# Splitting the low parts of the last stage's weights between VectorE and GpSimd

## The chip, the cores and the metric

The kernel runs on one core of a Trainium2 chip. The metric is the device time of one execution in microseconds (us), the median over runs. Engines are named as the profile names them: PE is TensorE's matrix multiply and PEld its weight load, DVE is VectorE, ACT is ScalarE, POOL is GpSimd, SP is SyncE. In the trace each engine's instructions start in the order of its own list, so one that waits for another engine holds up everything behind it in that list.

## What is computed

One layer of a bidirectional encoder: an input projection, windowed attention, a bidirectional state-space scan, and then the last stage, which the change touches. Cut to that stage (x, h, attn, y and z_ssm come from the stages before; S = 2048 rows, D = 1024):

```python
y = jax.nn.gelu(y)
y = y * jax.nn.sigmoid(jnp.einsum('bsc,ce->bse', y, w_glu[l]) + b_glu[l])
ssm = y * jax.nn.silu(z_ssm)
merged = jax.nn.sigmoid(g_attn) * jnp.einsum('bsc,cd->bsd', attn, w_branch_attn[l]) \
       + jax.nn.sigmoid(g_ssm) * jnp.einsum('bsc,cd->bsd', ssm, w_branch_ssm[l])
x = x + jnp.einsum('bsd,de->bse', merged, w_out[l])
return rms_norm(x, final_norm_gain)
```

## The kernel before, in words

Every product is made in three passes (`mm3`, from line 218). Each operand is split into a high part, which is the value rounded to the matrix type, and a low part, which is the value minus the high part; then high times high, low activation times high weight, and high activation times low weight are added in one PSUM bank (lines 221, 222, 223). So every weight that PE uses needs a high part `wh` and a low part `wl` first. `split_w` (line 158) makes them: a DMA on SP's queue brings a tile `raw` of 128 x 1024, ACT copies it to `wh` (line 164), and `low_part` (line 150) subtracts `wh` from `raw` into `wl`. Before the change `low_part` does that on GpSimd in four instructions of 128x256 (line 156), except for the very first weight of the last stage, which VectorE does in one of 128x1024. There are two `raw` buffers and three pairs of `wh` and `wl`.

The last stage runs over four blocks of 512 rows in the order 2, 3, 1, 0; the text calls them the first, second, third and last block. A block has three parts.

- `glu`: four groups of 12 matmuls with `w_glu`, each followed by elementwise work on VectorE (`g`, `g`, `ta`, `sl`) and ACT (`ta`, `sh`).
- `branch`: for each e from 0 to 7 two groups of 12 matmuls, n = 0 with the attention weights (`ah`, `al`, bank `pj`) and n = 1 with the state-space weights (`sh`, `sl`, bank `s`). One weight tile holds both: its first half (columns k 0 to 3) is n = 0's, its second half n = 1's. After a group VectorE takes its bank out into a gate tile `gt` (line 1435); after n = 1 it adds the two (`m`, line 1439), ACT makes `mh` (line 1440) and VectorE the low part `ml` (line 1448).
- `outp`: eight groups of 24 matmuls with the output weight `woh`, `wol`, each followed by the residual add `xr` on VectorE (line 1491), then the final norm and the store.

The order is written out by hand. `wahead` (line 210) keeps the split weights ahead of PE: in `branch` the weight of e + 2 is split right behind the group (e, 0). While a branch runs, a side generator, `gelu_prep`, prepares the next block's `gh` and `gl` one step per group: a load of `yt` by ACT's DMA queue, a square on ACT (line 1321), a multiply on VectorE (line 1325), a tanh on ACT (line 1329), a multiply on VectorE (line 1333), the copy `gh` on ACT (line 1334) and the low part `gl` on VectorE (line 1338). The next block's `glu` needs all four `gl`. The last block has no such side work.

The output weight has two halves of 512 columns. The first is split before the first `glu`. The second is split inside the first block's `branch` in eight pieces (`wo_split`, line 1161): ACT makes `woh` and, as `WOP` is 1, GpSimd makes `wol` in two instructions of 128x256 (line 1173).

Of the kernel before, what the change touches and what calls it, by code (L numbers as in the profile page):

```python
# [7 lines left out]
F32 = mybir.dt.float32  # L8
# [4 lines left out]
ALU = mybir.AluOpType  # L13
# [6 lines left out]
KD = 8  # L20
# [7 lines left out]
RATE2 = 1.237  # L28
RATE3 = 1.499
WLAG = 2  # L30
WOP = 1
GELU_Q = 0.044715 ** 0.5
SCAN_SLOT = 0.994
FIRST = 1.711
# [4 lines left out]
def kernel(  # L39
# [10 lines left out]
    V, A, Q, PE = nc.vector, nc.scalar, nc.gpsimd, nc.tensor  # L50
# [49 lines left out]
    HALF = "half"  # L100
# [3 lines left out]
    def later(n, f):  # L104
        laters.append((n, f))
# [44 lines left out]
    def low_part(eng, lo, r, hi):  # L150

        n = lo.shape[1]
        step = max(1, n // 4) if eng is Q else n
        for k in range(0, n, step):
            ks = slice(k, k + step)
            eng.tensor_tensor(lo[:, ks], r[:, ks], hi[:, ks].bitcast(F32), ALU.subtract)  # L156

    def split_w(key, kt, cols, tag="w", bufs=3, eng=Q):
        r = wraw.pop(key)
        res = []  # L160
        for nm in ("h", "l"):
            t = wp.tile([128, KD, 128], F32R, tag=tag + nm, name=tag + nm, bufs=bufs)
            res.append(t.rearrange("p k c -> p (k c)")[:, 0:kt * cols].rearrange("p (k c) -> p k c", k=kt))
        A.activation(res[0], r, AF.Copy)  # L164
        low_part(eng, res[1], r, res[0])
        return res

    witems = []
    wsplit = []
    wpos = {"load": 0, "split": 0, "lag": WLAG}  # L170

    def wload_to(i):
        while wpos["load"] <= min(i, len(witems) - 1):
            r = wp.tile([128, KD, 128], F32, tag="raw", name="raw", bufs=2)
            it = witems[wpos["load"]]
            k0 = 0
            if it[0] == "h":
                nc.sync.dma_start(out=r.rearrange("p k c -> p (k c)").rearrange("p (k c) -> p k c", k=2),
                                  in_=hS[it[1], :, it[2]:it[2] + 2])
            elif it[0] == "wo":  # L180
                wo_load(0, it[1], r.rearrange("p k c -> p (k c)").rearrange("p (k c) -> p k c", k=2))
            for src in it[:0 if it[0] in ("wo", "h") else len(it)]:
                kt = src.shape[0] // 128
                nc.sync.dma_start(out=r[:, k0:k0 + kt], in_=src.rearrange("(k p) c -> p k c", p=128))
                k0 += kt
            wraw[wpos["load"]] = r
            wpos["load"] += 1

    def wsplit_next():
        j = wpos["split"]  # L190
        wload_to(j)
        it = witems[j]
        if it[0] == "h":
            h_split(it[1], it[2], wraw.pop(j).rearrange("p k c -> p (k c)").rearrange("p (k c) -> p k c", k=2))
        elif it[0] == "wo":
            wo_split(0, it[1], wraw.pop(j).rearrange("p k c -> p (k c)").rearrange("p (k c) -> p k c", k=2), V)
        else:
            wsplit.append(split_w(j, KD, 128, eng=V if j == wpos["glu"] else Q))
        wpos["split"] += 1
        if wpos["lag"]:  # L200
            later(wpos["lag"], lambda: wload_to(j + 2))
        else:
            wload_to(j + 2)
# [6 lines left out]
    def wahead(n):  # L210
        while len(wsplit) < n and wpos["split"] < len(witems):
            wsplit_next()

    def wpre():
        wload_to(1)
        wsplit_next()
# [921 lines left out]
    with tc.manual_schedule():  # L1138
# [11 lines left out]
        def h_split(b, k, r):  # L1150
            if k == 0:
                hblk[b] = [hp.tile([128, KD, BLK], F32R, tag=t, name=t) for t in ("hh", "hl")]
            hh, hl = hblk[b]
            ks = slice(k, k + 2)
            A.activation(hh[:, ks], r, AF.Copy)
            for j in range(2):
                for c in range(2):
                    cs = slice(c * 256, (c + 1) * 256)
                    Q.tensor_tensor(hl[:, k + j, cs], r[:, j, cs], hh[:, k + j, cs].bitcast(F32), ALU.subtract)

        def wo_split(n, k, r, eng):
            if (0, n) not in wo:
                wo[0, n] = hp.tile([128, KD, BLK], F32R, tag="hh", name="woh")
                wo[1, n] = hp.tile([128, KD, BLK], F32R, tag="hl", name="wol")
            ks = slice(k, k + r.shape[1])
            A.activation(wo[0, n][:, ks], r, AF.Copy)
            if eng is V:
                V.tensor_tensor(wo[1, n][:, ks], r, wo[0, n][:, ks].bitcast(F32), ALU.subtract)
                return
            for j in range(r.shape[1]):  # L1170
                for c in range(2):
                    cs = slice(c * 256, (c + 1) * 256)
                    Q.tensor_tensor(wo[1, n][:, k + j, cs], r[:, j, cs], wo[0, n][:, k + j, cs].bitcast(F32), ALU.subtract)
# [25 lines left out]
        def wsplit1(key):  # L1199
            if len(wt) < 3:  # L1200
                wt[key] = split_w(key, KD, 128)
                return
            r = wraw.pop(key)
            th = wI.tile([128, KD, 128], F32R, name=f"wh{key[0]}{key[1]}")
            tl = wI.tile([128, KD, 128], F32R, name=f"wl{key[0]}{key[1]}")
            A.activation(th, r, AF.Copy)
            low_part(Q, tl, r, th)
            wt[key] = (th, tl)
# [213 lines left out]
        def branch(b, nxt):  # L1422
# [6 lines left out]
            for e, n in seq:  # L1429
# [22 lines left out]
                if b == BO[0]:  # L1452
# [4 lines left out]
                    elif sl % 4 >= 2:  # L1457
                        k = sl // 4 * 2 + sl % 4 - 2
                        wo_split(1, k, wor[:, k % 2:k % 2 + 1], Q if WOP else V)
                if (e, n) == (1, 0):  # L1460
# [90 lines left out]
        for b in (2, 3, 0, 1):  # L1551
            for n, (key, w) in enumerate(zip(shared, ws)):
                for _ in range((2, 1, 1)[n] if b in (3, 0) else b == 1 and n == 1):
                    wsplit_next()
                proj(key[0], key[1], b, w)
# [82 lines left out]
```

## Time and profile before

| what | value |
|---|---|
| median of 3 runs | 1527.67 us (1526.7 to 1529.14) |
| the profiled execution | 1530.28 us, of which its span is 1528.5 us |
| PE busy | 1423.8 us, 93% of the span |
| DVE busy | 1027.4 us, 67% |
| ACT busy | 644.7 us, 42% |
| POOL busy | 629.1 us, 41% |
| mean granted TensorE clock | 0.975 |
| the last stage | from about 1087 us to the end |

The page counts busy time by engine over the whole span. The last stage is 441 us of it; of GpSimd's 380 weight instructions of line 156, 156 start there. Shares over the span say little about a stage: the views below are taken for stretches of it.

### The profile page before, as it was taken

How to read it: one execution, taken by the hardware profiler on the slowest of the kernel's cores; microseconds unless marked ns; L12 is line 12 of the kernel's file. 1: busy time of each engine (PE TensorE's matmuls, PEld its weight loads, DVE VectorE, ACT ScalarE, POOL GpSimd, SP SyncE). 2: the span in 40 equal slices, each digit the busy share in tenths (PEclk: the TensorE clock that was granted, in tenths of full speed). 3: DMA queues.
4: the chain of work that ended last, by engine and by line, in shares of the span. 5: the costliest groups of instructions: out<-in, count | busy, mean ns of one | idle time of the engine just before them, and what ended most of it. 6: DMA issues, size and time to landing. Idle time of an engine off the chain costs nothing.

```text
span 1528.5 us, 20091 instructions
## 1 busy us (share of the span) xinstructions
PE 1423.8 (93%) x6933; PEld 1154.0 (75%) x6933; DVE 1027.4 (67%) x2145; ACT 644.7 (42%) x1165; POOL 629.1 (41%) x887
## 2 busy tenths in 40 slices
PE   7999959988899999799999999999988998999998
PEld 6787747767777777688878888888766786877886
DVE  3325607899889998927888988863577376386442
ACT  6332123343344434424666666654444143243111
POOL 5520366966777861723111111113367053153320
PEclk9999979999999999999999999999999999999999
DMA  7443212232232233454323233235576376375341
GB/s 263 152 109 89 77 62 87 85 98 87 74 106 94 89 100 97 148 153 133 94 87 94 90 101 94 89 111 154 179 205 183 120 186 180 111 187 182 111 125 69
DMA packets 240727, 185.51 MB, mean 121 GB/s; under 512 B 57921, under 2 KB 202433, under 8 KB 240625
## 3 DMA queue, kind: packets, MB, share of 16 engines
q10 hardware_dynamic: 108336, 100.61, 22.5%
q1 hardware_dynamic: 132288, 83.62, 18.4%
q8 instruction: 54, 0.88, 0.2%
q14 instruction: 49, 0.39, 0.1%
HBM read 126.56 MB, written 57.62 MB: 121 GB/s over the span
## 4 chain that ended last, share of the span: by engine, by line
PE 46%; DVE 19%; DMA 8%; POOL 6%; issue 5%; ACT 4%; ACTq 0%; SPq 0%; POOLq 0%; DVEq 0%
PE pj L221 9%; PE pj L223 9%; PE pj L222 9%; DVE Hl L811 3%; PE s L1484 3%; PE s L1485 3%; PE s L1486 3%; PE s L1055 2%; PE s L1002 2%; PE s L1039 2%; DMA yt<-yS 2%; POOL wl L156 2%; DMA ar<-aS 2%; DVE ft L784 1%; DVE fu L785 1%
## 5 line engine op out<-in xcount | busy, mean ns | idle before, releaser
L156 POOL TENSOR_TENSOR wl<-raw,wh 128x256 fp32r<-128x256 f32 x380 | 329.8, 899 | 597.8 <-ACT wh L164 586.2
L221 PE MATMUL pj<-hh,wh 128*128 128x512 f32 x976 | 395.4, 405 | 0.0
L223 PE MATMUL pj<-hh,wl 128*128 128x512 f32 x976 | 387.5, 397 | 5.3 <-POOL wl L156 5.3
L222 PE MATMUL pj<-hl,wh 128*128 128x512 f32 x976 | 386.8, 396 | 0.0
L223 PEld LDWEIGHTS pj<-hh,wl 128*128 128x128 f32 x976 | 186.5, 191 | 48.2 <-POOL wl L156 6.6
L221 PEld LDWEIGHTS pj<-hh,wh 128*128 128x128 f32 x976 | 187.6, 192 | 36.7 <-issue 3.6
L222 PEld LDWEIGHTS pj<-hl,wh 128*128 128x128 f32 x976 | 187.5, 192 | 33.8
L164 ACT ACTIVATE wh<-raw 128x1024 fp32r<-128x1024 f32 x96 | 100.7, 1051 | 19.9 <-DMA raw<-in_w_branch_ssm_dram 5.7
L1484 PE MATMUL s<-woh,mh 128*128 128x512 f32 x256 | 101.9, 398 | 6.4 <-DVE xr L1491 6.4
L1486 PE MATMUL s<-woh,ml 128*128 128x512 f32 x256 | 101.3, 396 | 0.0
L1485 PE MATMUL s<-wol,mh 128*128 128x512 f32 x256 | 101.2, 395 | 0.0
L405 ACT ACTIVATE st<-pj,bg 128x512 f32<-128x512 f32 x64 | 44.0, 687 | 98.7 <-PE pj L223 86.8
L1019 ACT ACTIVATE p<-p,sml 128x384 f32<-128x384 f32 (+1 forms) x128 | 75.8, 595 | 17.4 <-DVE sml L1015 17.4
L1042 ACT ACTIVATE ph<-s 128x512 fp32r<-128x512 f32 x92 | 54.3, 590 | 57.5 <-PE s L1039 57.5
L1528 POOL TENSOR_TENSOR sm<-sm,mhalf 128x1 f32<-128x1 f32 x15 | 8.3, 553 | 170.3 <-DVE sm L1527 133.7
L1003 DVE CUSTOM_DVE_ANT_0 p<-s,bias 128x384 f32<-128x384 f32 (+1 forms) x128 | 68.3, 533 | 12.6 <-PE s L1002 12.0
L1044 DVE TENSOR_TENSOR pl<-s,ph 128x512 fp32r<-128x512 f32 x92 | 63.2, 687 | 19.2 <-ACT ph L1042 17.8
L1491 DVE TENSOR_TENSOR xr<-xr,s 128x512 f32<-128x512 f32 x32 | 21.9, 684 | 68.9 <-PE s L1486 68.9
L1484 PEld LDWEIGHTS s<-woh,mh 128*128 128x128 f32 x256 | 48.1, 188 | 20.4 <-DVE xr L1491 9.1
L1002 PE MATMUL s<-kst,qs 128*128 128x384 f32 (+1 forms) x256 | 61.7, 342 | 0.6 <-issue 0.6
L1039 PE MATMUL s<-ident,p 128*128 128x128 f32 x368 | 57.6, 274 | 0.0
L1039 PEld LDWEIGHTS s<-ident,p 128*128 128x128 f32 x368 | 46.4, 140 | 14.7 <-DVE p L1031 2.2
(277 smaller groups left out, 3038.5 us busy)
## 6 DMA issues: line engine op xcount, KB each, us to landing
raw<-in_w_in_dram SPq DMA_DIRECT2D x59, 512.0 KB
gS<-st ACTq DMA_DIRECT2D x64, 256.0 KB
gt<-gS ACTq DMA_DIRECT2D x64, 256.0 KB
x<-in_x_dram SPq DMA_DIRECT2D x16, 512.0 KB
raw<-in_w_branch_attn_dram SPq DMA_DIRECT2D x32, 256.0 KB
raw<-in_w_branch_ssm_dram SPq DMA_DIRECT2D x32, 256.0 KB
out_dram<-xr ACTq DMA_DIRECT2D x15, 512.0 KB
xr<-in_x_dram SPq DMA_DIRECT2D x12, 512.0 KB
```

What stands on the lines that cost most here:

```text
L156: eng.tensor_tensor(lo[:, ks], r[:, ks], hi[:, ks].bitcast(F32), ALU.subtract)
L164: A.activation(res[0], r, AF.Copy)
L221: PE.matmul(pt, w[0][:, k], r[0][:, k], start=start and k == 0, stop=False)
L222: PE.matmul(pt, w[0][:, k], r[1][:, k], start=False, stop=False)
L223: PE.matmul(pt, w[1][:, k], r[0][:, k], start=False, stop=stop and k == kt - 1)
L1002: PE.matmul(pt[:, 0:w], s["qs"][:, h], kst[:, r, kv, k0 * 128:k1 * 128], start=r == 0, stop=r == 1)
L1003: V.tensor_tensor_reduce(out=p[:, h, 0:w], in0=pt[:, 0:w], in1=bias[:, kv * 4 + h, r0:r1:-1], scale=1.0, scalar=0.0, op0=ALU.add, op1=ALU. ...
L1019: A.activation(p[:, h, 0:w], p[:, h, 0:w], AF.Exp, bias=nm[:, j:j + 1], accum_out=den[:, j:j + 1])
L1039: PE.transpose(pt[:, h * 128:(h + 1) * 128], s["p"][:, h, i * 128:(i + 1) * 128], ident)
L1484: PE.matmul(pt, mh[k][:, ts_], wo[0, n][:, k], start=k == 0, stop=False)
L1485: PE.matmul(pt, mh[k][:, ts_], wo[1, n][:, k], start=False, stop=False)
L1486: PE.matmul(pt, ml[k][:, ts_], wo[0, n][:, k], start=False, stop=k == KD - 1)
```

## The change

`low_part` gets a third kind, "half": VectorE subtracts the first half of the tile in one instruction of 128x512, and GpSimd the second half in two of 128x256. All weights of the last stage behind the first one are made that way (39 tiles: one of `w_glu` in the first block, two in each other, and eight of the branch weights in each of the four). `WOP` becomes 0, so that VectorE makes the eight pieces of the output weight's second half, in one instruction of 128x512 each.

```diff
-WOP = 1
+WOP = 0
...
         n = lo.shape[1]
-        step = max(1, n // 4) if eng is Q else n
-        for k in range(0, n, step):
+        if eng is HALF:
+            ks = slice(0, n // 2)
+            V.tensor_tensor(lo[:, ks], r[:, ks], hi[:, ks].bitcast(F32), ALU.subtract)
+        step = max(1, n // 4) if eng is not V else n
+        for k in range(n // 2 if eng is HALF else 0, n, step):
             ks = slice(k, k + step)
-            eng.tensor_tensor(lo[:, ks], r[:, ks], hi[:, ks].bitcast(F32), ALU.subtract)
+            (V if eng is V else Q).tensor_tensor(lo[:, ks], r[:, ks], hi[:, ks].bitcast(F32), ALU.subtract)
...
-            wsplit.append(split_w(j, KD, 128, eng=V if j == wpos["glu"] else Q))
+            wsplit.append(split_w(j, KD, 128, eng=V if j == wpos["glu"] else HALF if j > wpos["glu"] else Q))
```

Lines from 160 on stand three lines later in the changed file. The lists of PE, ACT and SP hold the same instructions in the same order as before; those of VectorE and GpSimd change.

VectorE in the second block's branch, from the bank of (2, 0) on. In the names, `gt` with `pj` is the bank of an n = 0 group taken out, with `s1` that of an n = 1 group; `yt` and `gl` are the side work for the next block. Before:

```order
L1435 SCALAR_TENSOR_TENSOR gt_11959<-gt_11959,pj_11999 128x512
L1338 TENSOR_TENSOR gl_11902<-yt_11903,gh_11901 128x512
L1435 SCALAR_TENSOR_TENSOR gt_11961<-gt_11961,s1_12025 128x512
L1439 TENSOR_TENSOR m_12041<-gt_11959,gt_11961 128x512
L1448 SCALAR_TENSOR_TENSOR ml_11884<-m_12041,mh_11876 128x512
L1325 SCALAR_TENSOR_TENSOR yt_11905<-yt_11905 128x512
L1435 SCALAR_TENSOR_TENSOR gt_11994<-gt_11994,pj_12049 128x512
L1333 SCALAR_TENSOR_TENSOR yt_11905<-yt_11905 128x512
```

The same place now:

```order
L1438 SCALAR_TENSOR_TENSOR gt_11937<-gt_11937,pj_11976 128x512
L155 TENSOR_TENSOR wl_11993<-raw_11916,wh_11992 128x512
L1341 TENSOR_TENSOR gl_11881<-yt_11882,gh_11880 128x512
L1438 SCALAR_TENSOR_TENSOR gt_11939<-gt_11939,s1_12001 128x512
L1442 TENSOR_TENSOR m_12017<-gt_11937,gt_11939 128x512
L1451 SCALAR_TENSOR_TENSOR ml_11863<-m_12017,mh_11855 128x512
L1328 SCALAR_TENSOR_TENSOR yt_11884<-yt_11884 128x512
L1438 SCALAR_TENSOR_TENSOR gt_11971<-gt_11971,pj_12025 128x512
L155 TENSOR_TENSOR wl_12042<-raw_11949,wh_12041 128x512
L1336 SCALAR_TENSOR_TENSOR yt_11884<-yt_11884 128x512
```

Behind each bank of an n = 0 group VectorE now has a low part, which reads the `wh` that ACT has still to make; everything below it, the side work among it, comes after.

ACT's list at the same place, which is unchanged (rows of the changed program; DMA issues stand among them):

```order
L1337 ACTIVATE gh_11880<-yt_11882 128x512
L167 ACTIVATE wh_11992<-raw_11916 128x1024
L1324 ACTIVATE yt_11884<-yt_11884 128x512
L1443 ACTIVATE mh_11855<-m_12017 128x512
```

`wh` stands behind `gh`, which itself reads the `yt` that VectorE made just before. GpSimd in the first block's branch, before:

```order
L156 TENSOR_TENSOR wl_11107<-raw_10968,wh_11106 128x256 x4
L1173 TENSOR_TENSOR wol_11140<-wor_11090,woh_11139 128x256 x2
L156 TENSOR_TENSOR wl_11145<-raw_11001,wh_11144 128x256 x4
L1173 TENSOR_TENSOR wol_11140<-wor_11090,woh_11139 128x256 x2
L156 TENSOR_TENSOR wl_11200<-raw_11113,wh_11199 128x256 x4
```

and now:

```order
L159 TENSOR_TENSOR wl_11104<-raw_10966,wh_11103 128x256 x2
L159 TENSOR_TENSOR wl_11140<-raw_10998,wh_11139 128x256 x2
L159 TENSOR_TENSOR wl_11193<-raw_11109,wh_11192 128x256 x2
L159 TENSOR_TENSOR wl_11244<-raw_11145,wh_11243 128x256 x2
L159 TENSOR_TENSOR wl_11299<-raw_11198,wh_11298 128x256 x2
```

The pieces of the output weight are gone from GpSimd, and two of four instructions of each weight; VectorE's list there has a `wol` and a `wl` more for each e.

## Rows read from the trace of the kernel before

**Rows 1.** The page's first section: busy us (share of the span) and number of instructions of each engine.

```profile
PE 1423.8 (93%) x6933; PEld 1154.0 (75%) x6933; DVE 1027.4 (67%) x2145; ACT 644.7 (42%) x1165; POOL 629.1 (41%) x887
```

**Rows 2.** The windows view of three branches (first, second and last block): the stretch, its length, then busy us and number of instructions of PE, PEld, DVE, ACT and POOL, then the granted clock, the DMA share and GB/s.

```profile
1113.00:1165.00 52.00, 45.74 (x176) 33.67 (x176) 39.70 (x43) 25.74 (x37) 41.96 (x45) 0.95 0.77 205
...
1222.00:1271.00 49.00, 46.13 (x196) 36.20 (x195) 37.56 (x45) 21.68 (x27) 26.92 (x32) 1.00 0.73 180
...
1434.00:1478.00 44.00, 44.00 (x191) 35.33 (x190) 23.58 (x33) 10.89 (x15) 20.82 (x25) 1.00 0.64 167
```

**Rows 3.** The waits view of PE from 1085 us to the end: who waited for whom, us in total, times, longest.

```profile
PE s L1484 <- DVE xr L1491: 6.4, 6, 2.0
PE pj L222 <- DVE gl L1338: 4.5, 3, 1.6
PE pj L221 <- ACT wh L164: 3.8, 6, 1.2
PE pj L223 <- POOL wl L156: 2.7, 2, 1.3
```

**Rows 4.** The same view and stretch for PE's weight loads.

```profile
PEld pj L223 <- POOL wl L156: 6.3, 7, 1.8
```

**Rows 5.** The timeline of VectorE in the second block's branch: start us, us, instruction, number, and in brackets the idle time before it and what ended it. Only some rows of the stretch.

```profile
1236.33 0.67 DVE L1435 SCALAR_TENSOR_TENSOR gt<-gt,pj 128x512 f32<-128x512 f32 x1
...
1242.76 0.68 DVE L1435 SCALAR_TENSOR_TENSOR gt<-gt,pj 128x512 f32<-128x512 f32 x1
...
1255.22 0.68 DVE L1435 SCALAR_TENSOR_TENSOR gt<-gt,pj 128x512 f32<-128x512 f32 x1
...
1261.75 0.69 DVE L1448 SCALAR_TENSOR_TENSOR ml<-m,mh 128x512 fp32r<-128x512 f32 x1 [3.40 <-ACT mh L1440]
1262.36 1.08 DVE L1325 SCALAR_TENSOR_TENSOR yt<-yt 128x512 f32<-128x512 f32 x1
1263.36 0.67 DVE L1435 SCALAR_TENSOR_TENSOR gt<-gt,pj 128x512 f32<-128x512 f32 x1
1264.14 1.05 DVE L1333 SCALAR_TENSOR_TENSOR yt<-yt 128x512 f32<-128x512 f32 x1
...
1268.86 0.68 DVE L1338 TENSOR_TENSOR gl<-yt,gh 128x512 fp32r<-128x512 f32 x1
```

**Rows 6.** The timeline of ACT in the same stretch, the weight copies and one row of the side work.

```profile
1237.03 1.05 ACT L164 ACTIVATE wh<-raw 128x1024 fp32r<-128x1024 f32 x1
...
1243.41 1.05 ACT L164 ACTIVATE wh<-raw 128x1024 fp32r<-128x1024 f32 x1
...
1255.94 1.04 ACT L164 ACTIVATE wh<-raw 128x1024 fp32r<-128x1024 f32 x1
1260.07 1.12 ACT L1321 ACTIVATE yt<-yt 128x512 f32<-128x512 f32 x1 [3.09 <-DMA yt<-yS]
...
1264.01 1.04 ACT L164 ACTIVATE wh<-raw 128x1024 fp32r<-128x1024 f32 x1
```

**Rows 7.** The timeline of PE at the seam between the second block's branch and the third block's glu.

```profile
1265.11 0.50 PE L221 MATMUL pj<-gh,wh 128*128 128x512 f32 x1 [1.23 <-ACT wh L164]
...
1269.60 0.51 PE L222 MATMUL pj<-gl,wh 128*128 128x512 f32 x1 [1.56 <-DVE gl L1338]
```

**Rows 8.** The view of one line, for three lines: instructions, duration in ns as least/median/most, first and last start, form.

```profile
L156 POOL TENSOR_TENSOR wl<-raw,wh x380: 718/747/1790, 9.9 to 1466.8; 128x256 fp32r<-128x256 f32 x190
...
L1439 DVE TENSOR_TENSOR m<-gt x32: 691/926/1279, 1116.7 to 1477.7; 128x512 f32<-128x512 f32 x32
...
L1448 DVE SCALAR_TENSOR_TENSOR ml<-m,mh x32: 691/1144/1154, 1120.0 to 1479.1; 128x512 fp32r<-128x512 f32 x32
...
L1435 DVE SCALAR_TENSOR_TENSOR gt<-gt,s x32: 671/680/689, 1116.0 to 1477.0; 128x512 f32<-128x512 f32 x32
```

**Rows 9.** The lines view of VectorE from 1222 to 1271 us (second block's branch): group, number, busy us, mean ns of one, idle before.

```profile
L1439 DVE TENSOR_TENSOR m<-gt 128x512 f32<-128x512 f32 x8 | 8.0, 1005 | 0.3
L1448 DVE SCALAR_TENSOR_TENSOR ml<-m,mh 128x512 fp32r<-128x512 f32 x7 | 7.1, 1014 | 7.7 <-ACT mh L1440 7.7
...
L1325 DVE SCALAR_TENSOR_TENSOR yt<-yt 128x512 f32<-128x512 f32 x4 | 4.9, 1226 | 0.0
L1333 DVE SCALAR_TENSOR_TENSOR yt<-yt 128x512 f32<-128x512 f32 x4 | 4.9, 1216 | 0.2
```

**Rows 10.** The same view from 1113 to 1165 us (first block's branch).

```profile
L1448 DVE SCALAR_TENSOR_TENSOR ml<-m,mh 128x512 fp32r<-128x512 f32 x8 | 8.5, 1063 | 9.1 <-ACT mh L1440 9.1
L1439 DVE TENSOR_TENSOR m<-gt 128x512 f32<-128x512 f32 x8 | 8.2, 1025 | 0.3
...
L1333 DVE SCALAR_TENSOR_TENSOR yt<-yt 128x512 f32<-128x512 f32 x4 | 5.4, 1355 | 0.2
L1325 DVE SCALAR_TENSOR_TENSOR yt<-yt 128x512 f32<-128x512 f32 x4 | 5.4, 1342 | 0.0
...
L1338 DVE TENSOR_TENSOR gl<-yt,gh 128x512 fp32r<-128x512 f32 x4 | 4.2, 1055 | 0.3 <-ACT gh L1334 0.3
```

**Rows 11.** The timeline of PE in the first block's branch, at a wait for a low part and behind it.

```profile
1138.30 0.64 PE L223 MATMUL pj<-ah,wl 128*128 128x512 f32 x1 [1.35 <-POOL wl L156]
1138.74 0.63 PE L221 MATMUL pj<-ah,wh 128*128 128x512 f32 x1
...
1141.73 0.48 PE L222 MATMUL pj<-al,wh 128*128 128x512 f32 x1
1142.05 0.40 PE L223 MATMUL pj<-ah,wl 128*128 128x512 f32 x1
1142.28 0.40 PE L221 MATMUL s<-sh,wh 128*128 128x512 f32 x1
```

## The prediction

> **What bounds the kernel now.** The page's first section comes first: over the span PE is busy 93% of the time, VectorE 67% and GpSimd 41% [rows 1]. These are averages, so the next view is the windows view of three branches [rows 2]. A branch is 16 groups of 12 matmuls; in the last block, where PE has no gap, it takes 44.0 us for 191 recorded matmuls, 0.23 us each. The first branch takes 52 us and the second 49. So PE loses some 8 us in the first branch and 5 about the second. There VectorE is busy 39.7 of 52 and 37.6 of 49 us, but only 23.6 of 44 in the last block, which has no side work.
>
> Who ends PE's waits in the last stage? The output product's adds 6.4 us, `gl` 4.5, `wh` 3.8, and GpSimd's low parts 2.7 [rows 3]; on the weight loads, which run ahead, GpSimd's low parts end 6.3 us in seven waits [rows 4]. So what the change relieves is at most some 6 us; the two largest waits are for VectorE, which it loads.
>
> The timeline of VectorE and ACT in the second branch shows how far behind VectorE is. At the seam PE is in the next glu at 1265.11 and waits at 1269.60 for `gl` [rows 7], which VectorE makes from 1268.86 to 1269.54 [rows 5]; the bank of (6, 0) was taken out only at 1263.36, when PE had left the branch. VectorE's list, with its ping-pong with ACT, is the chain that sets when the next glu can go on. Whatever is put into it ahead of the last `gl` moves that seam.
>
> **The change part by part.** *Price of a low part on VectorE.* The same form, two SBUF inputs and 128x512, takes 0.691 us at the least; the medians are 0.926 and 1.144 [rows 8]. The instructions that take one input from PSUM keep to 0.67 to 0.69 [rows 8]. So something slows the ones with two SBUF inputs alone; GpSimd's weight pieces, which run beside them, are spread as well, from 0.718 to 1.790 us, and I take the two to slow each other. GpSimd's two pieces of a tile wait for the same `wh` as VectorE's half, so both start together: I take 1.1 us, near the upper row (ends 0.69 and 1.15). For the output weight's pieces, which GpSimd no longer does, I take 0.7.
>
> *The wait that is added.* VectorE's half stands right behind the bank of (e, 0), and reads a `wh` that ACT makes behind `gh` or a tanh, which themselves waited for VectorE. In the old timeline the banks end at 1237.00, 1243.44, 1255.90 and 1264.03 [rows 5], and the `wh` that would follow end at 1238.08, 1244.46, 1256.98 and 1265.05 [rows 6]: 1.1, 1.0, 1.1 and 1.0 us in which VectorE would stand. GpSimd stood there before, with nothing behind it that mattered. Six tiles come ahead of the last `gl` (e = 3 to 7 and the next glu's first); I take five such waits of 1.0, since one may find its `wh` ready (ends 4 and 6.2). Behind the waiting instruction stand `gl`, the n = 1 bank, `m` and the side work; ACT's `mh`, tanh and next `wh` wait for those, and PE for `wh` and `gl`.
>
> *What is given back.* GpSimd runs two pieces a tile where it ran four. The excess of VectorE's instructions over the bare ones in the second branch is 8 x (1.005 - 0.691) for `m`, 7 x (1.014 - 0.691) for `ml`, and 4 x (1.226 - 1.08) and 4 x (1.216 - 1.05) for the two `yt` [rows 5, 8, 9]: 2.5, 2.3, 0.6 and 0.7, in all 6.1 us. Half of GpSimd's pieces go, and one of the two left runs beside the low part that I have priced as slowed, so I take three quarters, 4.6 (ends 2 and 6.1). VectorE also stood 3.4 us for an `mh` behind ACT's square, which waited for the load of `yt` [rows 5, 6]. That load is issued behind `mh` of e = 4, which shifts too, so only about 1 us of it absorbs anything (ends 0 and 3.4).
>
> *Second and third block, each.* 6 x 1.1 + 5 x 1.0 - 4.6 - 1 = 6.0 us later at the last `gl`. In glu and outp two more low parts with short waits stand against less slowing; I take 0.5 (ends -0.5 and 1.5). With the ends: -1.4 - 0.5 = -2 and 6.9 + 6.2 - 2 + 1.5 = 12.6. Sum: 6.5 each, 13 for both.
>
> *First block.* The same six low parts, 6.6 us, six `wol` ahead of the last `gl`, 4.2, waits on `woh` and `wh` together 4 (ends 2 and 6; a `wol` fills part of the time to `wh`), and 1.5 from the three low parts in the glu before, ahead of `sl`. The excess there is larger: 8 x 0.334 + 8 x 0.372 for `m` and `ml`, 4 x 0.305 + 4 x 0.262 for `yt`, 4 x 0.375 for `gl` (bare 0.68), 9.4 us [rows 5, 8, 10]; with 16 GpSimd pieces left of 45 [rows 2] I take back 7 (ends 3 and 9.4), and 1 absorbed. 6.6 + 4.2 + 4 + 1.5 - 7 - 1 = 8.3, and 0.2 in outp: 8.5. The ends are -2.5 and 17. PE's waits for GpSimd's low parts, nearly all in this branch, do go; but PE then only comes earlier to a seam that VectorE sets, so I count them as nothing. If VectorE had slack, they would be a gain: that is the first rival.
>
> *Last block.* No side work; VectorE is busy 23.6 of 44 us [rows 2]. Eight low parts with their waits, some 16 us, fit: 0. Other engines' lists and the DMAs are unchanged; `raw` buffers come free when both halves are done, near where GpSimd's fourth piece ended before: 0.
>
> *The sum.* 8.5 + 13 = 21.5 us on the profiled execution's 1530.28, which is 1551.8. That execution was 2.6 us above the median of 1527.67, so the forecast is 1549.2.
>
> **The rivals.** *VectorE has room, and GpSimd was the limit (faster).* GpSimd's low parts end 6.3 us of PE's weight loads' waits [rows 4], and behind one of them PE ran at steps of 0.43 us from 1138.74 to 1141.73, half rate, against 0.23 [rows 11]: some 1.4 us more over seven steps. Without both: 1527.67 - 7.7 = 1520.0. It decides if the waits for `wh` come to under some 0.6 us a tile, so that per block no more is added than the slowing that goes (6.1) and the square's wait absorbs (3.4). For it: bare, GpSimd needs 2 x 0.718 us for what VectorE does in 0.691 [rows 8]. Against it: the rows of `wh` above. The Trainium skill's page "SBUF — State Buffer", section "Who interferes with whom", says that VectorE instructions with two SBUF inputs and GpSimd's contend for a pair of ports that is an exclusive lock. By that rule the pair's bare work in the first branch, 45 x 0.718 = 32.3 of GpSimd and 22.3 of VectorE, 54.6 us in 52, would itself be the bound, and 11.5 + 33.4 = 44.9 us would remain: the sum would be 7 us faster there. The trace speaks half for it: the slowing is there, but 54.6 us of work in 52 must have overlapped a little. I give the rival 0.13.
>
> *It cancels.* The first branch gains its 5 to 8 us, the other two lose theirs at the low end: 1525 to 1530, taken as 1527.5. VectorE's 12.3 and 11.4 us of idle time in these branches [rows 2] speak for it, but 9.1 and 7.7 of that are its waits for `mh` [rows 9, 10], into which nothing behind can be pulled. 0.09.
>
> *The clock falls too.* The granted clock was 0.95 in the first branch against 1.00 in the second [rows 2], and the half-rate steps came behind waits of over a microsecond [rows 11]. Where PE waits at every e, more such spells could come: eight, at 1.4 us, would give 1560. But PE that waits for VectorE has time to be slow. 0.04. That the change does not do what it says is excluded by the order of the lists: VectorE gets 39 + 8 instructions.
>
> **How the numbers follow.** The forecast has 0.74, the rivals 0.13, 0.09 and 0.04. Below about 0.2%, 3 us, a measurement of this kernel cannot tell a difference from none. The terms' ends add to -6.5 and +42 us; all at one end together is unlikely, and the lower ones are the rivals' ground. Of the forecast I keep 1531 to 1562; taking in the second rival the range is 1527 to 1562, which leaves out the faster rival and a little at both ends. Slower: 0.74 and 0.04, 0.78. Same: 0.09. Faster: 0.13.
>
> **What would show it.** Right: in the branch of the second block VectorE waits for ACT's `wh` some 1 us at each low part and these take about 1.1 us; `m` and `ml` fall from 1.0 us toward 0.8; PE's waits for GpSimd's low parts are gone and those for `wh`, VectorE's `wl` and `gl` have grown; the second branch takes some 55 us instead of 49, the last one 44 as before. Wrong: low parts of 0.7 us without waits, or branches no longer than now.

## The result and the profile after

| | before | after |
|---|---|---|
| median | 1527.18 us, 4 runs (1526.42 to 1529.14) | 1549.84 us, 4 runs (1547.21 to 1550.5) |
| ratio | | 1.0143, 95% interval 1.0126 to 1.0161 |
| the profiled execution | 1530.28 us, span 1528.5 | 1549.27 us, span 1547.5 |
| mean granted clock | 0.975 | 0.967 |

The changed kernel is 22.7 us slower by the medians; 1549.2 was forecast. The profiled executions differ by 19.0 us.

Where the time went is read from the seams. A seam is the point at the end of a block's branch where PE, already in the next block's glu, starts the first matmul that reads the last `gl` (k = 3); for the last block it is the last matmul of all. The seam's distance from the one before it (for the first block, from the stage's first `gh` matmul) was 74.4, 107.9, 106.4 and 145.4 us before; after the change it is 81.1, 114.0, 112.8 and 147.1. That is 6.6, 6.2, 6.5 and 1.7 us more, in all 21.0; the last stage itself began 1.9 us earlier in this execution.

The page's engines line of the changed kernel, against [rows 1]: VectorE gained 16 us, GpSimd lost 69, ACT is unchanged.

```profile
PE 1438.2 (93%) x6933; PEld 1162.6 (75%) x6933; DVE 1043.5 (67%) x2192; ACT 644.4 (42%) x1165; POOL 559.9 (36%) x793
```

The windows view of three stretches about the first, second and last block's branch, columns as in [rows 2]. The last branch is as full of matmuls as before (191 in 44.0 us). In the first two GpSimd has a third and a half of its instructions, and PE's mean granted clock is lower (0.94 and 0.97, for 0.95 and 1.00).

```profile
1111.00:1164.00 53.00, 45.05 (x169) 33.09 (x169) 39.65 (x52) 23.04 (x32) 17.39 (x14) 0.94 0.69 191
1224.00:1277.00 53.00, 50.99 (x208) 39.49 (x208) 36.06 (x46) 20.59 (x26) 17.25 (x15) 0.97 0.59 161
1453.00:1497.00 44.00, 44.00 (x191) 35.33 (x190) 27.23 (x39) 10.91 (x15) 11.67 (x13) 1.00 0.61 167
```

PE's waits in the last stage, against [rows 3]; the last row is the weight loads', against [rows 4]. No row for GpSimd's low parts is left. The waits for `wh` and `gl` went from 3.8 and 4.5 us to 9.7 and 6.3.

```profile
PE pj L224 <- ACT wh L167: 9.7, 8, 2.0
PE s L1487 <- DVE xr L1494: 7.0, 3, 2.3
PE pj L225 <- DVE gl L1341: 6.3, 3, 2.1
...
PEld pj L226 <- DVE wl L155: 6.0, 12, 1.8
```

VectorE's timeline in the second branch, as [rows 5]. These two low parts wait 1.26 and 1.11 us for `wh` and then take a bare 0.69, the least that the form takes in [rows 8]; the side work behind them is what comes out stretched (1.62, 1.23). `m` and `ml` are bare.

```profile
1238.43 0.69 DVE L155 TENSOR_TENSOR wl<-raw,wh 128x512 fp32r<-128x512 f32 x1 [1.26 <-ACT wh L167]
1239.05 1.62 DVE L1328 SCALAR_TENSOR_TENSOR yt<-yt 128x512 f32<-128x512 f32 x1
1240.59 0.68 DVE L1438 SCALAR_TENSOR_TENSOR gt<-gt,s 128x512 f32<-128x512 f32 x1
1241.30 0.69 DVE L1442 TENSOR_TENSOR m<-gt 128x512 f32<-128x512 f32 x1
1242.69 0.69 DVE L1451 SCALAR_TENSOR_TENSOR ml<-m,mh 128x512 fp32r<-128x512 f32 x1 [0.70 <-ACT mh L1443]
1243.30 1.08 DVE L1336 SCALAR_TENSOR_TENSOR yt<-yt 128x512 f32<-128x512 f32 x1
1244.31 0.68 DVE L1438 SCALAR_TENSOR_TENSOR gt<-gt,pj 128x512 f32<-128x512 f32 x1
1246.09 0.69 DVE L155 TENSOR_TENSOR wl<-raw,wh 128x512 fp32r<-128x512 f32 x1 [1.11 <-ACT wh L167]
1246.70 1.23 DVE L1341 TENSOR_TENSOR gl<-yt,gh 128x512 fp32r<-128x512 f32 x1
```

ACT's list at the second of these two low parts, as [rows 6]. Here the cycle is closed: `gh` waits for VectorE's `yt` (1243.30 above), `wh` stands behind `gh`, and VectorE then waits for `wh`.

```profile
1244.48 0.63 ACT L1337 ACTIVATE gh<-yt 128x512 fp32r<-128x512 f32 x1 [1.82 <-DVE yt L1336]
1245.02 1.04 ACT L167 ACTIVATE wh<-raw 128x1024 fp32r<-128x1024 f32 x1
```

All that VectorE waited for from 1237.2 to 1280.4 us, the changed second branch from the end of its first `ml` to its seam: not once for PE.

```profile
DVE wl L155 <- ACT wh L167: 6.0, 6, 1.3
DVE ml L1451 <- ACT mh L1443: 4.2, 6, 0.8
```

And in the kernel before, from 1230.4 to 1269.6 us:

```profile
DVE ml L1448 <- ACT mh L1440: 6.9, 6, 3.4
```

ACT's waits show one way by which PE reaches VectorE's list in this stretch: the `wh` at its start waits for a matmul of PE, and the low part of 1238.43 waits for that `wh`. That wait of ACT is as long as before the change (the changed kernel's row, then the kernel before's), so what PE loses inside this stretch to its clock or its own waits is not what moved this seam.

```profile
ACT wh L167 <- PE s L226: 0.9, 1, 0.9
```

```profile
ACT wh L164 <- PE s L223: 0.9, 1, 0.9
```

PE at that seam, where it waits 2.09 us for `gl`; in [rows 7] it was 1.56:

```profile
1280.45 0.50 PE L225 MATMUL pj<-gl,wh 128*128 128x512 f32 x1 [2.09 <-DVE gl L1341]
```

VectorE's groups in the whole last stage (number, busy us, mean ns, idle before), and behind them `m` and `ml` in the kernel before. Their means fall from 938 and 983 ns to 736 and 693.

```profile
L155 DVE TENSOR_TENSOR wl<-raw,wh 128x512 fp32r<-128x512 f32 x39 | 28.0, 718 | 19.6 <-ACT wh L167 19.2 <-DMA gt<-gS 0.3
L1442 DVE TENSOR_TENSOR m<-gt 128x512 f32<-128x512 f32 x32 | 23.5, 736 | 1.1
L1451 DVE SCALAR_TENSOR_TENSOR ml<-m,mh 128x512 fp32r<-128x512 f32 x32 | 22.2, 693 | 24.0 <-ACT mh L1443 24.0
```

```profile
L1448 DVE SCALAR_TENSOR_TENSOR ml<-m,mh 128x512 fp32r<-128x512 f32 x32 | 31.5, 983 | 31.3 <-ACT mh L1440 31.3
L1439 DVE TENSOR_TENSOR m<-gt 128x512 f32<-128x512 f32 x32 | 30.0, 938 | 1.1
```

PE in the first block's outp. Behind a wait of 2.29 us its matmuls start 0.59 and then 0.43 us apart, the half-rate steps of [rows 11] in another place (from 1190.29 us on the granted clock is 0.50 for 3.4 us, the lower of its two levels, 1.2 of 2.4 GHz; such a stretch is called a spell below).

```profile
1190.57 0.80 PE L1487 MATMUL s<-woh,mh 128*128 128x512 f32 x1 [2.29 <-DVE xr L1494]
1191.16 0.63 PE L1488 MATMUL s<-wol,mh 128*128 128x512 f32 x1
1191.59 0.63 PE L1489 MATMUL s<-woh,ml 128*128 128x512 f32 x1
```

### The profile page after: what moved, and what is told of

Its sections match the earlier page's. It is cut to its first block, busy times and chain, and to the rows that moved or that the text cites. A ratio compares the mean times of both kernels' runs of the same rounds, so it can differ in the third digit from the quotient of the medians.

```text
span 1547.5 us, 20097 instructions
## 1 busy us (share of the span) xinstructions
PE 1438.2 (93%) x6933; PEld 1162.6 (75%) x6933; DVE 1043.5 (67%) x2192; ACT 644.4 (42%) x1165; POOL 559.9 (36%) x793
## 3 DMA queue, kind: packets, MB, share of 16 engines
q10 hardware_dynamic: 108336, 100.61, 21.5%
## 4 chain that ended last, share of the span: by engine, by line
PE 43%; DVE 17%; POOL 11%; issue 8%; ACT 5%; DMA 5%; ACTq 1%; SPq 0%; POOLq 0%; DVEq 0%
PE pj L224 8%; PE pj L226 8%; PE pj L225 7%; PE s L1487 3%; PE s L1488 3%; PE s L1489 3%; POOL t L639 3%; POOL t L640 3%; POOL wl L159 2%; PE s L1058 2%; PE s L1005 2%; PE s L1042 2%; DMA yt<-yS 2%; ACT wh L167 2%; POOL wt L641 2%
## 5 line engine op out<-in xcount | busy, mean ns | idle before, releaser
L159 POOL TENSOR_TENSOR wl<-raw,wh 128x256 fp32r<-128x256 f32 x302 | 276.9, 945 | 688.5 <-ACT wh L167 685.0
L1047 DVE TENSOR_TENSOR pl<-s,ph 128x512 fp32r<-128x512 f32 x92 | 63.3, 688 | 19.2 <-ACT ph L1045 17.8
L224 PE MATMUL pj<-ah,wh 128*128 128x512 f32 x128 | 54.1, 423 | 11.3 <-ACT wh L167 8.9
L1487 PEld LDWEIGHTS s<-woh,mh 128*128 128x128 f32 x256 | 49.2, 192 | 20.3 <-DVE xr L1494 8.5
L1488 PEld LDWEIGHTS s<-wol,mh 128*128 128x128 f32 x256 | 49.4, 193 | 11.7
```

What stands on the lines that cost most here:

```text
L159: (V if eng is V else Q).tensor_tensor(lo[:, ks], r[:, ks], hi[:, ks].bitcast(F32), ALU.subtract)
L224: PE.matmul(pt, w[0][:, k], r[0][:, k], start=start and k == 0, stop=False)
L1047: return lambda: V.tensor_tensor(pl, pt, ph.bitcast(F32), ALU.subtract)
L1487: PE.matmul(pt, mh[k][:, ts_], wo[0, n][:, k], start=k == 0, stop=False)
L1488: PE.matmul(pt, mh[k][:, ts_], wo[1, n][:, k], start=False, stop=False)
```

## The experiments

The theory, T1: VectorE's list sets the seams, and the change costs time by what it adds there, work and in-order waits (waits for another engine that hold up all that stands behind them in the list). R1 is the rival to it, in the form that each expectation gives; R2 puts the time on the half-rate clock. Medians stand beside those of the kernel before on the same chip; distances between seams are those of the one profiled execution.

### The wait alone, and its control

The kernel before, with one more VectorE instruction of 128x1 that reads the new `wh`, ahead of the call that makes `wl`, where the changed kernel has VectorE's half. It runs for all 39 tiles (38 of them have a record), first in place, then one group later. The diff shows the first, with the casts cut (`...`).

```diff
+        if tiny:
+            V.tensor_tensor(tiny[0], res[0][:, 0, 0:1]..., res[0][:, 0, 1:2]..., ALU.add)
         low_part(eng, res[1], r, res[0])
```

The control has the same line inside `later(1, lambda: ...)`.

> The kernel before, plus one VectorE instruction of 128x1 that reads each new wh of the last stage, at the place where the changed kernel has its half of the low part. All low parts stay on GpSimd. VectorE gets the wait for wh and next to no work. T1 (the in-order wait is a cost of its own): some 1 us of wait at each of six tiles a block, less the 3.4 us wait for mh that absorbs part of it, and GpSimd's four pieces slow the instruction behind as before: 3 to 5 us later at each of the first three seams, 1537 to 1543 us. R1 (only the added work counts, the wait falls into time that VectorE would have stood anyway): within 3 us of before, 1524 to 1530.

> The control of the run with the wait alone: the same 39 instructions of 128x1 reading each new wh on VectorE, but one group later, between m and ml, where wh has long been made. T1 (the wait for wh at that place costs, not an instruction more): 1525 to 1530 us, as before. R1 (39 more instructions with their semaphores cost by themselves): well over it, up to the 22 us of the run with the wait.

Measured in place: 1548.96 against 1526.49 us, ratio 1.0144 (1.0129 to 1.0158). One group later: 1527.48 against 1527.46, ratio 1.0003 (0.999 to 1.0017). In place the first three distances are 5.9, 6.8 and 7.1 us longer than before, as in the changed kernel. T1's 3 to 5 us a seam, 1537 to 1543 us, was too low; R1 is out in both runs. The timelines of VectorE in the second branch, first in place, then later:

```profile
1242.85 0.68 DVE L1438 SCALAR_TENSOR_TENSOR gt<-gt,pj 128x512 f32<-128x512 f32 x1
1244.64 0.16 DVE L167 TENSOR_TENSOR tiny<-wh 128x1 f32<-128x1 f32 x1 [1.11 <-ACT wh L165]
1244.72 1.26 DVE L1341 TENSOR_TENSOR gl<-yt,gh 128x512 fp32r<-128x512 f32 x1
```

```profile
1235.60 0.96 DVE L1442 TENSOR_TENSOR m<-gt 128x512 f32<-128x512 f32 x1
1236.48 0.70 DVE L167 TENSOR_TENSOR tiny<-wh 128x1 f32<-128x1 f32 x1
1237.26 1.15 DVE L1451 SCALAR_TENSOR_TENSOR ml<-m,mh 128x512 fp32r<-128x512 f32 x1
```

VectorE's waits at the new instruction in place, over the stage; one group later it has none.

```profile
DVE tiny L167 <- ACT wh L165: 24.7, 27, 1.7
```

One element a partition, with a wait of 24.7 us in 27 places, costs what the whole change costs. Behind `m` the same instruction falls where VectorE stood for `mh` anyway.

### The same work without the wait

The changed kernel, VectorE's half one group later, between `m` and `ml`.

```diff
-            V.tensor_tensor(lo[:, ks], r[:, ks], hi[:, ks].bitcast(F32), ALU.subtract)
+            later(1, lambda ks=ks: V.tensor_tensor(lo[:, ks], r[:, ks], hi[:, ks].bitcast(F32), ALU.subtract))
```

> The changed kernel with VectorE's half issued one group later: it then stands between m and ml of the same e, where VectorE waits 0.7 us for mh anyway, and its wh has long been made. Same work, same GpSimd pieces, no wait for wh. T1 (the wait for wh and the place make the loss, not the amount of work): the half of 0.69 us fills a wait of 0.70, the seams of the second and third block come back by most of their 6 us; six wol remain in the first: 1527 to 1533 us, and below before (1522 to 1526) if the freed GpSimd also relieves VectorE's slowed instructions. R1 (the added work makes the loss): 1543 to 1550. R2 (half-rate spells come from PE's waits): they fall back to two or three with the seams.

1532.56 against 1526.49 us, ratio 1.0041 (1.0027 to 1.0054): by the ratios some 16 of the 22 us are gone while the work remained, so R1 is out. VectorE's waits for `wh` at a low part fell from 19.2 to 6.2 us. The four distances are 80.4, 105.4, 109.4 and 143.1: the second and the last are shorter than before, the third is 3.1 longer, and the first stays 6.0 longer. PE now waits for something else, the low part itself, which comes a group later; 12.5 of these 17.5 us lie ahead of the first seam:

```profile
PE pj L226 <- DVE wl L155: 17.5, 11, 3.3
PE pj L224 <- ACT wh L167: 3.4, 3, 1.8
```

### Twice the work, the same wait

```diff
+            for _ in range(2):
                 V.tensor_tensor(lo[:, ks], r[:, ks], hi[:, ks].bitcast(F32), ALU.subtract)
```

> The changed kernel with VectorE's half of the low part done twice, the second time over the same data: 39 more instructions of 0.69 us (up to 1.2 us where GpSimd's pieces run beside them) and no further wait. T1 (every added microsecond on VectorE's list ahead of a seam moves the seam one for one): six a block ahead of the last gl, 4 to 7 us at each of the first three seams: 12 to 20 us over the changed kernel, 1562 to 1570. R1 (the waits alone cost, work of 0.7 us finds room): 0 to 5 us over it.

1579.13 us, 29.3 over the changed kernel (ratio to before 1.0344, 1.033 to 1.0357); its group of 78 low parts is busy 69.5 us where 39 took 28.0. In the second branch, from the end of the first `ml` to the start of the last `gl`, VectorE's list is 6.7 us longer than the changed kernel's (49.2 for 42.5), and there each of the six low parts is 1.13 us longer, 6.8 in all: one for one. The distances to the first three seams grew by 5.3, 10.4 and 9.2 us over the changed kernel's and the last by 3.8. `wl` itself is now late for PE:

```profile
PE pj L227 <- DVE wl L156: 17.6, 18, 1.1
PE s L1488 <- DVE xr L1495: 11.4, 3, 4.4
```

The changed kernel has 1.4 us of the first kind, once. None of the 18 waits lies in the last block, whose branch has room even for twice the work; the 3.8 us are the third block's outp, where the wait for `xr` is now 3.4 us. So work counts where VectorE is full. T1's 12 to 20 us were too low, since they left out glu and outp. What is lost there is not VectorE's alone for certain: the half-rate length ahead of the tail is sixteen spells here, nine in the changed kernel, and its share was not separated.

### The two parts of the change apart

One run is the changed kernel with `WOP = 1`, the other the kernel before with `WOP = 0`.

> The halves of the low parts alone; the output weight's pieces stay on GpSimd. They are split only in the first block, so the second and third seam distances should be those of the changed kernel, 6 us longer than before each, under every theory. T1 (VectorE's list, added work and waits for wh, sets each seam): the six wol of 0.7 us (4.2 us) leave VectorE's list in the first block, so its seam comes 3 to 5 us earlier than in the changed kernel, where it was 6.6 later than before: some 1545 us. R1 (the output weight on VectorE costs nothing or helps, because GpSimd is freed): within 1 us of the changed kernel or slower, 1549 to 1552. R2 (the clock's half-rate spells make most of the time): the time follows their number in the last stage (2 before, 9 in the changed kernel, each 3.4 us long and at most 1.7 us dearer), whatever VectorE has to do.

> The output weight's pieces on VectorE alone; the weights' low parts stay on GpSimd. T1: six pieces of 0.7 us stand in VectorE's list ahead of the first block's last gl, less what GpSimd's missing 16 pieces of up to 1.8 us no longer slow; 0 to 4 us slower than before, all of it in the first block: 1527 to 1531 us. R1 (GpSimd is the limit in the first branch): its low parts no longer stand behind 16 pieces of the output weight, PE's waits for them (6.3 us of weight loads' waits) go and the kernel is 3 to 6 us faster than before: 1521 to 1524.

The halves alone: 1547.67 against 1526.75 us, ratio 1.0133 (1.011 to 1.0157), distances 80.2, 114.0, 112.7 and 147.3. The output weight alone: 1528.28, ratio 1.0012 (0.9998 to 1.0026), first distance 73.0 instead of 74.4. The halves are the loss. The six `wol` ahead of the first seam cost 0.8 us there by these two executions, and by themselves nothing that can be told (the first distance is also 73.1 in the control of the wait, so it varies by over 1 us by itself): neither T1's 3 to 5 us nor the gain that R1 looked for in the second run. Their work is there, but from 1098 us to the first seam VectorE's waits for `wh` are 3.1 us with them and 6.0 without: a `wol` stands where VectorE would have waited. The runs say nothing on R2: the halves alone have the changed kernel's nine half-rate spells and its time.

### The weights split a group earlier

The second run does to the kernel before what the first does to the changed one.

```diff
                 if n == 0:
                     ws[e] = wnext(0)
+                    if e >= 2:
+                        wahead(2)
...
-                elif (e, n) == (0, 1) or e >= 2 and n == 0:
+                elif (e, n) == (0, 1):
```

> The changed kernel, with the weight of e + 2 split ahead of the matmuls of (e, 0) instead of behind them: wh then stands in ACT's list ahead of that group's work and the half of wl in VectorE's list ahead of the bank of (e, 0). The amount of added work is the same; only the place differs. In the second branch VectorE waited 6.04 us for wh at six low parts that themselves took 6 x 0.69 = 4.1 us. T1 (the in-order wait behind wh makes more than half of the loss): the mean wait falls from 1.0 to 0.3 or 0.4 us, each of the first three seams comes some 3 to 4 us earlier: 1538 to 1542 us. R1 (the added work and its slowing make the loss, the wait falls into time that VectorE had to spare): 1547 to 1551, unchanged. R2 (half-rate spells): the time falls only as far as their number does, seven fewer being worth at most 11 us.

> The kernel before with the weight of e + 2 split ahead of the matmuls of (e, 0) instead of behind them; all low parts stay on GpSimd. It is the base for the run that does this to the changed kernel: what the earlier place does by itself. T1: VectorE's list is the same as before, and ACT's wh of 0.7 us stands ahead of mh or a tanh by at most one place; PE's waits for wh (3.8 us) and for GpSimd's low parts (2.7 us, 6.3 on the weight loads) shrink, but the seams are VectorE's: -3 to +2 us, 1524 to 1529. R1 (VectorE has room, late weights are the limit): 5 to 8 us faster, 1519 to 1522. If the earlier wh delays mh, VectorE's list grows by up to 0.7 us a group and the seams come up to 4 us later each.

1547.79 (ratio 1.0137, 1.0113 to 1.0161) and 1534.99 us (1.006, 1.0036 to 1.0084), both against 1526.75. Taken alone the first would speak for R1, but it did not do what it was made for:

```profile
1247.56 0.69 DVE L1453 SCALAR_TENSOR_TENSOR ml<-m,mh 128x512 fp32r<-128x512 f32 x1 [0.70 <-ACT mh L1445]
1248.98 0.69 DVE L155 TENSOR_TENSOR wl<-raw,wh 128x512 fp32r<-128x512 f32 x1 [0.73 <-ACT wh L167]
1249.59 1.63 DVE L1328 SCALAR_TENSOR_TENSOR yt<-yt 128x512 f32<-128x512 f32 x1
```

`wh` now follows `mh` in ACT's list, and VectorE, which has just waited for that `mh`, waits for `wh` behind it: 20.9 us in 35 places over the stage, where the changed kernel has 19.2. The wait was moved, not removed. In the kernel before the move costs 8 us by itself; PE's longest waits there are 4.1 us for `wh` and 4.0 for `xr`, and VectorE's waits for `mh` are 37.2 us where they were 31.3. This pair is inconclusive on T1, and why the earlier place costs 8 us I did not pursue.

### The opposite direction

The kernel before with `gl` made by GpSimd (`g4`, line 1338).

```diff
-                V.tensor_tensor(gl[:, e], ta, gh[:, e].bitcast(F32), ALU.subtract)
+                for c in range(2):
+                    cs = slice(c * 256, (c + 1) * 256)
+                    Q.tensor_tensor(gl[:, e, cs], ta[:, cs], gh[:, e, cs].bitcast(F32), ALU.subtract)
```

> The kernel before with the low part gl of the next block's activations made by GpSimd, in two instructions of 128x256, instead of by VectorE: four instructions of 0.7 to 1.3 us leave VectorE's list in each of the first three branches. The opposite direction of the change. T1 (VectorE's list sets the seams, GpSimd has room): 2 to 4 us earlier at each seam, unless GpSimd's gl, behind the pieces of a wl, is itself late by the 3 us that these take: 1517 to 1525 us. R1 (GpSimd is the limit): gl and the wl behind it come later and the kernel is 3 to 10 us slower, 1530 to 1537.

1530.23 against 1526.49 us, ratio 1.0018 (1.0009 to 1.0028). Taking four instructions a block from VectorE gained nothing: PE waits for `gl` as before, 2.3 instead of 1.5 us on average, now behind GpSimd.

```profile
PE pj L222 <- POOL gl L1340: 6.8, 3, 2.3
```

T1's gain did not come, and the time lies at the low end of R1's range. The first distance is 77.1, 2.7 us longer than before; ahead of that seam PE's waits for GpSimd's `wl` rose from 2.7 to 4.9 us. So in the first block, where GpSimd also makes `wol`, it seems to have had no room for more. The second and third distances are only 0.5 and 0.2 us shorter. The excuse that T1 carried, a `gl` behind the pieces of a `wl`, is what the row would look like, but I did not test it further.

### Towards a version that beats both

The run with the half one group later, cut to some tiles by the condition in `wsplit_next`; everything else stays on GpSimd.

```diff
-... HALF if j > wpos["glu"] else Q
+... HALF if j >= wpos["glu"] + 10 and (j - wpos["glu"]) % 10 >= 2 else Q        (first)
+... HALF if j >= wpos["glu"] + 14 and (j - wpos["glu"] - 12) % 10 >= 2 else Q   (second)
```

> The run with the half one group later, cut to where its profile shows that it paid: only the branch weights of the second, third and last block are halved that way; the weights of glu, ahead of each seam, and all of the first block stay on GpSimd; the output weight stays on VectorE. In that run the distance to the seam was 2.4 us shorter than before in the second block, 2.3 us shorter in the last, 3.1 longer in the third (with PE waiting 1.3 and 1.9 us for wl) and 6.0 longer in the first, where PE waited for wl seven times; with the output weight on VectorE alone the first was 1.4 us shorter. T1 (VectorE's list sets the seam, and the late wl of glu is what stands ahead of it now): -1.4, -2.4, 0 and -2.3 us, 1519 to 1523 us, faster than both kernels. R1 (the shorter distances came from the order in which PE and VectorE happened to meet behind a late first block): 1526 to 1531, no better than before.

> The run before it picked the tiles two places off: its profile shows VectorE's wl in glu, where PE waits 1.9 us for it at every seam, and none at the last two branch weights of a block. Here the halves, one group later, are those of the branch weights of the second, third and last block and no others; glu's weights and the whole first block stay on GpSimd, the output weight on VectorE. T1 (VectorE's list sets the seam, and a half between m and ml costs it nothing): the 1.9 us behind wl at the second and third seam go, GpSimd's two pieces a tile slow m, ml and yt less than four: the two middle distances 105 to 107 us instead of 107.9 and 106.4, the last 143 to 145 instead of 145.4: 1520 to 1525 us. R1 (what is taken off one list comes back in another wait at the seam, now for gl or wh): 1526 to 1530, the same as before.

The first picked the wrong tiles, since two tiles of the output weight stand ahead of the second glu weight in the list: it halved the two glu weights and the first six branch weights of a block. 1528.65 against 1527.46 us, ratio 1.0006 (0.9995 to 1.0016). The second, with the tiles that were meant: 1531.9 against 1527.24, ratio 1.0028 (1.0018 to 1.0039), distances 74.7, 109.0, 108.8 and 145.6. T1's gain came in neither. The first is R1's time; the second lies 1.9 us above R1's range and is a little slower than before, most of it in the third distance (2.5 us), which I did not follow up. PE at the second seam, in the first and then in the second of these kernels:

```profile
1264.80 0.50 PE L226 MATMUL pj<-gh,wl 128*128 128x512 f32 x1 [1.91 <-DVE wl L155]
```

```profile
1264.66 0.50 PE L224 MATMUL pj<-gh,wh 128*128 128x512 f32 x1 [1.28 <-ACT wh L167]
1269.16 0.50 PE L225 MATMUL pj<-gl,wh 128*128 128x512 f32 x1 [1.55 <-DVE gl L1341]
```

With glu's `wl` off VectorE, as in the second of them, `wh` and `gl` are the late ones again, as in [rows 7]. No kernel of this study beats the one before.

### The clock

The windows view of the whole last stage, columns as in [rows 2]: the changed kernel, the first of the two above, and the control of the wait, one fence each.

```profile
1085.00:1540.00 455.00, 425.12 (x1729) 331.56 (x1728) 261.44 (x350) 137.79 (x193) 99.26 (x93) 0.97 0.50 147
```

```profile
1085.00:1520.00 435.00, 416.87 (x1730) 328.76 (x1728) 254.25 (x335) 138.03 (x193) 105.24 (x123) 0.98 0.53 153
```

```profile
1085.00:1518.00 433.00, 414.89 (x1731) 328.05 (x1729) 263.50 (x341) 137.79 (x193) 166.12 (x187) 0.98 0.54 153
```

The kernel before has 0.99 there and two half-rate spells of 3.4 us ahead of the tail; the changed kernel has nine. The other two have six and five spells' length of it, 20 and 17 us, and run as fast as before. The run with the wait in place has eight, three more than its control, and is 21.5 us slower than it; at half rate a spell can cost no more than half its 3.4 us, 1.7 each. So R2 is not the main cause.

Its share is open. From a seam to the first matmul of the next branch, glu and outp, PE took 57.2, 56.1 and 56.0 us before and takes 59.3, 57.8 and 57.7: 5.5 of the 21.0 us. PE's waits for `xr` there are 6.4 us before and 7.0 after. Before, there were two of them in each outp and no spell; now there is one longer wait, and behind it a spell of some 1.5 us, where the second wait of 0.9 to 1.2 us stood. What those three spells cost beyond the wait that they stand for was not isolated.

## Why the prediction was right

**What bounds the kernel.** That VectorE's list with its ping-pong with ACT sets the seam was right for additions: a wait put into it moves the seam by as much as the change does, and the same instruction in a hole of it costs nothing. The reading that PE loses 8 us in the first branch and 5 about the second was not: the stretches of [rows 2] are not the branches. By PE's matmuls the second branch took 45.0 us before, from 1218.92 to 1263.88, as the last one does, and the first 57.9; what PE lost about the second it lost at the seam and in outp. The sign of 55 us instead of 49 for the second branch is to be read so too: it is 49.6 us now, 4.6 longer, and the last 45.0 as before. Taking work out is another matter: `gl` on GpSimd gained nothing, since the seam then waited for GpSimd. Several chains end close together there.

**The terms in the second block's branch**, from the end of the first `ml` to the start of the last `gl`. The stretch was 38.5 us (1230.37 to 1268.86) and is 42.5 (1237.17 to 1279.71): 4.0 longer, where I had 6.0.
- Low parts: 6 x 0.69 = 4.1 us, not 6.6. I took the slowed price, and made low parts of about 1.1 us a sign of being right; the trace shows the bare price and puts the slowing on the next instruction.
- Wait for `wh`: 6.0, not 5.0. All six tiles waited, one of them 0.46 us.
- Given back: the excess over bare durations is 5.9 us before (2.5 `m`, 2.3 `ml`, 1.1 `yt`) and 3.3 after (2.2 `yt`, 1.1 `gl`): 2.6, not 4.6. `m` and `ml` did fall to bare, but the slowing moved to the side work.
- Absorbed: VectorE's waits for `mh` fell from 6.9 to 4.2 us, 2.7 instead of 1: the one of 3.4 us behind ACT's square [rows 5, 6] became one of 0.7.
- Together 4.1 + 6.0 - 2.6 - 2.7 = 4.8; the 4.0 read from the start times is less, since neighbouring records overlap by some 0.08 us.

**glu and outp.** I had 0.5 a block; from that seam of the first block to the end of the second's first `ml` it is 2.1 us (68.6 before, 70.8 after). One longer wait for `xr` with its half-rate steps, and a second spell in glu, are what stands there. Two mis-sized terms, -2 and +1.6, cancelled: the seam moved by 6.2, and 6.5 was forecast.

**First block.** 6.6 us, not 8.5. The output weight's 4.2 us of work are there, but they cost 0.8 by the run without them, since they stand in the wait for `wh`; VectorE's waits for `mh` absorbed 2.6 us (8.4 to 5.8) where I had 1, and `m`, `ml`, `yt` and `gl` gave back 5.6 (excess over the bare durations 8.9 to 3.3) where I had 7. **Last block.** 1.7 us, not 0: the distance holds the third block's outp, with one such `xr` wait and its spell; the branch itself is unchanged.

**How the sum comes about.** By the start times the branches, with the first glu, are 6.6, 4.1 and 4.8 us longer, where 8.3, 6.0 and 6.0 were forecast, and glu and outp behind them 5.5 where 1.2 was. So 20.3 + 1.2 was forecast and 15.5 + 5.5 came: the mechanism was right, the closeness of the total is luck. In the second branch the added work, 4.1 us, is paid by what is given back and absorbed, 5.3, and the wait is the net loss. The run with the wait alone shows that the wait is enough: GpSimd keeps all its pieces, next to nothing is added, `m` and `ml` are at 1088 and 820 ns instead of 736 and 693, and the time is the changed kernel's. That the work comes free over the whole stage is not shown: with it placed a group later 6 us are left.

**The rivals.** That VectorE has room was to be decided at 0.6 us of wait a tile; in the second branch it was 1.0, and the rival fell; in the first branch, with the `wol` in the list, the waits for `wh` were 3.1 us in all and its seam moved all the same. Its gain did appear (no wait for GpSimd's low parts is left) and was, as forecast, overtaken by the seam. GpSimd's two pieces beside the low part of 1238.43 take 2.80 us where bare they take 1.44, and `yt` behind takes 1.62 for 1.08, but the low part itself is not slowed. The Trainium skill's page "SBUF — State Buffer", section "Who interferes with whom", has an exclusive lock between the two, in which the order of issue decides who is held up. The trace agrees in this: the low part starts 0.05 us before the pieces and is bare, and the pieces and the `yt` behind it are the stretched ones. What spoke against the lock, 54.6 us of bare work in 52, is weaker than the prediction has it, since VectorE's neighbouring records overlap by some 0.08 us. That the clock falls too was half right: seven more spells came, as against the eight it priced, but not the 1560 us that were to follow from them. Those in the branches fall where VectorE sets the seam; what those in outp cost is open, as said above.

## What to carry to other kernels

An instruction that is moved to an in-order engine costs its wait before it costs its work: look up when its operand is ready, and where in that list the engine already stands for something else. Here 39 instructions of 0.16 us, most with some 0.9 us of wait in front, cost 22 us in the wrong place, and nothing measurable one group later. To test a suspected wait, put a tiny reader of the same operand into the old kernel at that place, and the same reader at a harmless place as its control.

## What was not expected of the hardware

Where VectorE's 128x512 low part and GpSimd's two pieces started within 0.05 us of each other, VectorE's took a bare 0.69 us in all six cases of the second branch, and the following instruction with SBUF inputs took 0.54 us more (1.62 to 1.64 for 1.08, 1.22 and 1.23 for 0.69). The slowing falls on the second instruction, not on the one that starts together. With the low part done twice the second one took 1.13 us, and the instruction behind it was stretched as well (1.60 to 1.63 for 1.08).

The 128x1 instruction is on record with 0.16 us behind a wait, but with 0.70 between `m` and `ml`, where `ml` begins as late as with its 0.70 us wait for `mh` before. The record seems to cover a stand that is booked as a wait elsewhere; why, no run shows.
